# Merge stage of a decoder layer: routing in steps between the next quarter's half column blocks, row weights applied on VectorE, output projection 512 columns wide

## The chip, the cores and the metric

The kernel runs on one core of a Trainium2 chip. The metric is the device time of one execution in microseconds (us), the median of several runs. The core has five engines that each work through their own list of instructions in order: TensorE (PE, matrix products; its weight loads are listed apart as PEld), VectorE (DVE), ScalarE (ACT), GpSimd (POOL) and SyncE (SP). An instruction waits at the head of its engine's list until the semaphores it names are set, and all behind it on that engine wait with it. Transfers are issued from an engine's list (here from SP and POOL) and run on the DMA engines.

## The reference, cut to what matters

One decoder layer over 2048 tokens of width 1024. Two token mixers run side by side, differential attention (`attn`) and a causal convolution module (`c`); gates merge them, and a hierarchical mixture of experts (4 groups of 8, top 1 group, top 2 experts) and a gated per-layer embedding follow:

```
y_a = attn.reshape(B, S, ATTN_WIDTH) @ w_attn_out[i]
y_b = c @ w_conv_out[i] + b_conv_out[i]
gates = jax.nn.sigmoid(g + b_gate[i])
merged = gates[..., :D] * y_a + gates[..., D:] * y_b
h = h + merged @ w_o[i]
t = rmsnorm(h, norm_ffn[i]).reshape(B * S, D)
moe = hierarchical_moe(t, w_router_group[i], b_router_group[i],
                       w_router_expert[i], b_router_expert[i], w1[i], w3[i], w2[i])
h = h + moe.reshape(B, S, D)
ple_gate = jax.nn.sigmoid(rmsnorm(h, norm_ple[i]) @ w_ple_gate[i] + b_ple_gate[i])
h = h + ple_gate * (p[i] @ w_ple_proj[i])
```

## The kernel before

The kernel has five stages: mix (input projection, convolution, gates), attention, merge, the experts (moe) and the embedding (ple). The change lies in merge, which runs from about 1216 to 1715 us, and in the last steps that prepare the experts' gather. Every large product is made from float32 split into a high and a low part (`split`: the high part by a copy on ACT, the low part by a subtraction on DVE, L91 and L92) and three products (`mm3`, L96 to L98: high x high, low x high, high x low).

**Merge** handles the tokens in 4 quarters of 512. For each quarter the inputs of both branches are loaded and split (`bah`/`bal` for attention, whose rows are also scaled by a broadcast product `aR`, and `bch`/`bcl` for convolution). Then come 8 column blocks `j` of 128 output columns. In each, PE makes two groups of 12 products 128x512, one for each branch, into an accumulator `mps` (3 buffers); DVE applies the gates (L738 to L740), and the merged block is split into `mh` (ACT) and `ml` (DVE). Weights come as units of 512 KB, loaded on SP into `eraw` and split into `ewh` and `ewl`; `fetch` takes the next unit ahead of its use (`MERGE_W` gives the number of raw and split buffers).

The second half of a quarter is the **output projection**: 4 column parts `cc` of 256, and for each 4 token tiles `t`, 24 products 128x256 into `mps`; DVE adds the result to the residual rows `hq` (L756), and ACT sums the squares (`junk`). Two steps later (`LOGITS_AFTER`, a list of things to do, `todo`) `logits` transposes pieces of `hq` (`tps`, `hT`) and makes the router's products `lp`.

Then `merge_tail` computes the norm weight `r` (`h_std`), the logits `L`, and writes the normed rows: for each of 4 tiles ACT copies `hq` times `r` into `tt` (two buffers, L810), POOL multiplies by the gain `gffn` (L811) and issues the store to `T` (L812); the 2 MB store of `hq` itself to `HD` (L813) goes the same queue. `route` is a long chain of small DVE operations (group maximum, first and second expert, L833 to L859), a prefix count on PE (`pre`, L862 to L864), codes and eight pairs of masks `oh` and `ob` on DVE (L886, L888), and eight products that add to the dispatch table `tab` (L889).

After the fourth quarter `pick` turns the table into the gather's index: copy `tabs`, transposes `tps` (L928), products `dps` (L933), then `free`, `dst` and `idx`, and POOL gathers rows `xs` from `T` (L1231). `project` makes 96 products `pps` of 128x512 for the last stage, which don't depend on the routing, and stores them as PJ from POOL (L969). The first product of the experts reads the gathered rows after transposes (`tps` L1246, `ups` L1269).

Merge is not written in the order in which it runs: a framework's scheduler places each instruction on its engine's list, by what it depends on and by its priority in program order, so code of one quarter can stand in the list among that of the next. From the experts on the order is a fixed table, and the change leaves it as it is.

## Time and profile before

| | us |
|---|---|
| median of 3 runs (lowest, highest) | 2820.81 (2819.80, 2825.62) |
| the profiled execution | 2816.46 |
| its span in the trace | 2814.7 |
| PE busy in the span | 2661.8 |
| DVE, ACT, POOL busy | 1986.5, 1471.0, 405.6 |

The time is that of a whole execution; the span runs from the first to the last instruction recorded, so 1.76 us lie around it. The engines work side by side, and busy times are not to be added. A busy time says little by itself: where two engines wait for each other in turn, neither is busy all the time.

### The profile page before, as it was taken

The numbers are of one execution on the slowest core, as the hardware profiler recorded it, in microseconds if no ns is written. First come the engines' busy times: TensorE is split into PE (matmuls) and PEld (weight loads), VectorE is DVE, ScalarE is ACT, GpSimd is POOL, SyncE is SP. The second block draws the span as 40 slices with busy tenths as digits, with TensorE's granted clock in tenths as the row PEclk, the third lists the DMA queues.
The fourth block names the chain that finished last, engine by engine and source line by source line (L and its number), as shares of the span: only waits on it lengthen the run. The fifth ranks groups of instructions, "written<-read, shape, count | busy, mean of one in ns | idle before, by whom it ended". The sixth has DMA issues, their size and how long they took to land. (4 is left out here: it accounts for less than half of the span.)

```text
span 2814.7 us, 38600 instructions
## 1 busy us (share of the span) xinstructions
PE 2661.8 (95%) x13910; PEld 2209.8 (79%) x13911; DVE 1986.5 (71%) x3006; ACT 1471.0 (52%) x2700; POOL 405.6 (14%) x311
## 2 busy tenths in 40 slices
PE   7999999999999999989999998999999999999897
PEld 5898977898778878879789796667667777777776
DVE  6996238997787888864856746577777777775454
ACT  5232344233666666644544435566766766665333
POOL 2011122023210000000110112111111211111121
PEclk9999999999999999999999998999999999999999
DMA  5133444134433324164745637778888887885462
GB/s 191 64 113 113 139 164 150 60 124 151 164 96 103 115 76 122 37 218 150 239 161 172 210 130 270 249 281 307 294 282 301 316 316 283 314 296 182 149 209 91
DMA packets 177828, 520.83 MB, mean 185 GB/s; under 512 B 19120, under 2 KB 48576, under 8 KB 177120
## 3 DMA queue, kind: packets, MB, share of 16 engines
q1 hardware_dynamic: 135536, 397.02, 42.2%
q0 software_dynamic: 23664, 83.54, 8.0%
q10 hardware_dynamic: 18432, 37.76, 3.5%
q8 instruction: 110, 1.80, 0.3%
q14 instruction: 86, 0.70, 0.1%
HBM read 417.58 MB, written 100.66 MB: 184 GB/s over the span
## 5 line engine op out<-in xcount | busy, mean ns | idle before, releaser
L92 DVE TENSOR_TENSOR ewl<-eraw,ewh 128x1024 fp32r<-128x1024 f32 x464 | 549.5, 1219 | 140.7 <-ACT ewh L91 138.5
L91 ACT ACTIVATE ewh<-eraw 128x1024 fp32r<-128x1024 f32 x464 | 468.5, 1052 | 64.6 <-PE mps L97 27.2
L387 DVE SCALAR_TENSOR_TENSOR co<-cb,pvt,co 128x1024 f32<-128x1024 f32 x240 | 312.2, 1338 | 1.6
L96 PE MATMUL ps<-uh,wh 128*128 128x512 f32 x576 | 232.4, 406 | 4.3 <-ACT uh L91 4.3
L586 DVE TENSOR_REDUCE nm<-sc 128x1 f32<-128x512 f32 (+3 forms) x320 | 185.0, 605 | 62.0 <-PE sc L583 47.9
L97 PE MATMUL ps<-ul,wh 128*128 128x512 f32 x576 | 228.5, 398 | 0.0
L98 PE MATMUL ps<-uh,wl 128*128 128x512 f32 x576 | 227.3, 396 | 0.0
L1269 PE MATMUL ups<-ewh,xt 128*128 128x512 f32 x480 | 194.7, 406 | 5.5 <-ACT ewh L91 5.3
L1270 PE MATMUL ups<-ewl,xt 128*128 128x512 f32 x480 | 189.5, 395 | 2.1 <-DVE ewl L92 2.1
L96 PE MATMUL ps<-wh,uh 128*128 128x384 f32 x512 | 173.0, 338 | 0.0
L98 PE MATMUL ps<-wh,ul 128*128 128x384 f32 x512 | 172.1, 336 | 0.0
L97 PE MATMUL ps<-wl,uh 128*128 128x384 f32 x512 | 172.0, 336 | 0.0
L1207 POOL DMA_INDIRECT Y<-y,dst x49 | 66.4, 1355 | 657.2 <-ACT y L1077 483.1
L96 PE MATMUL mps<-ewh,mh 128*128 128x256 f32 x512 | 149.8, 293 | 3.0 <-ACT mh L91 3.0
L97 PE MATMUL mps<-ewl,mh 128*128 128x256 f32 x512 | 145.3, 284 | 0.0
L98 PE MATMUL mps<-ewh,ml 128*128 128x256 f32 x512 | 144.8, 284 | 0.0
L96 PEld LDWEIGHTS ps<-uh,wh 128*128 128x128 f32 x576 | 109.0, 190 | 32.5 <-ACT uh L91 5.0
L97 PEld LDWEIGHTS ps<-ul,wh 128*128 128x128 f32 x576 | 109.1, 189 | 28.7 <-issue 1.9
L1272 PE MATMUL ups<-ewh,xt 128*128 128x512 f32 x480 | 129.6, 392 | 0.0
L98 PEld LDWEIGHTS ps<-uh,wl 128*128 128x128 f32 x576 | 108.7, 189 | 26.3
L582 PE MATMUL sc<-Kt,Qt 128*128 128x512 f32 (+2 forms) x320 | 126.3, 401 | 3.2 <-ACT pr L572 2.8
L91 ACT ACTIVATE ah<-tp 128x512 fp32r<-128x512 f32 x144 | 82.5, 603 | 82.3 <-PE tp L632 68.5
(338 smaller groups left out, 6922.1 us busy)
## 6 DMA issues: line engine op xcount, KB each, us to landing
eraw<-in_we SPq DMA_DIRECT2D x384, 512.0 KB, 5.4
G<-sg POOLq DMA_DIRECT2D x64, 256.0 KB, 2.9
eraw<-in_wac SPq DMA_DIRECT2D x32, 512.0 KB, 4.1
ga<-G SPq DMA_DIRECT2D x32, 512.0 KB, 4.9
eraw<-in_wo SPq DMA_DIRECT2D x32, 512.0 KB, 3.7
ys<-Y SPq DMA_DIRECT2D x32, 512.0 KB, 7.2
wraw<-in_wqkv SPq DMA_DIRECT2D x16, 768.0 KB, 4.4
wraw<-in_wg SPq DMA_DIRECT2D x20, 512.0 KB, 3.9
```

The costliest lines, as they stand in the source:

```text
L91: nc.scalar.activation(hi, x, AF.Copy)
L92: (lo_eng or nc.vector).tensor_tensor(lo, x, f32(hi), ALU.subtract)
L96: nc.tensor.matmul(ps, lh, rh, start=start, stop=False)
L97: nc.tensor.matmul(ps, lh, rl, start=False, stop=False)
L98: nc.tensor.matmul(ps, ll, rh, start=False, stop=stop)
L387: nc.vector.scalar_tensor_tensor(acc, cb[:, i : i + HALF], wi, acc, ALU.mult, ALU.add)
L582: nc.tensor.matmul(sc[:, :n], Qt[:, 2 * m, qs], ks, start=True, stop=False)
L586: nc.vector.tensor_reduce(nm[:, qi, m, c : c + 1], sc[:, :w], AX.X, ALU.max, negate=True)
L1207: self.nc.gpsimd.indirect_dma_start(out=self.Y[:, :], out_offset=bass.IndirectOffsetOnAxis(ap=dst[R], axis=0), in_=y[R], in_offset=None)
L1269: self.nc.tensor.matmul(ps, xt[:, k, :P], wk[0], start=k == 0, stop=False)
L1270: self.nc.tensor.matmul(ps, xt[:, k, :P], wk[1], start=False, stop=False)
L1272: self.nc.tensor.matmul(ps, xt[:, k, P:], wk[0], start=False, stop=k == NK - 1)
```

## The change

It has four parts.

1. The output projection makes products 512 columns wide: 2 column parts instead of 4, 24 products for each tile and part as before, into a full accumulator. The units of `wo` are cut another way for it, and the right operand of a product is two runs of 256 columns of one unit. `take` replaces `fetch`, and six split buffers replace five. `logits` is called for each tile and part, after one step instead of two.
2. `merge_tail`, `route`, `pick`, `project` and `projected` become generators. In the next quarter one step of routing is written after each of the two groups of a column block, and what is left of it before the next branch. In the last quarter routing and `pick` alternate with the steps of `project`.
3. The row store no longer uses ACT and POOL: one DVE operation (`rows_out`, L833 of the changed kernel) makes `tt` from `hq`, `r` and `gffn`. The store to `HD` is written ahead of those to `T`.
4. The capacities `caps`, 32 memsets on DVE in `pick`, are set once on POOL at the start.

```
@@ -39,8 +39,8 @@
 PR_BUFS = 11
 QK_AFTER = 10
 LN_AFTER = (4, 9)
-LOGITS_AFTER = 2
-MERGE_W = (2, 5)
+LOGITS_AFTER = 1
+MERGE_W = (2, 6)
 AHEAD = 5
 EARLY = 4
 MOE_W = (8, 14)
@@ -139,6 +139,9 @@
         self.idx = cp.tile([P, NBLK * NE], I32, name="idx")
         self.slots = cp.tile([1, 3, NE], I32, name="slots")
         self.over = cp.tile([1, 1], I32, name="over")
+        self.caps = cp.tile([1, NE], F32, name="caps")
+        for e in range(NE):
+            self.nc.gpsimd.memset(self.caps[:, e : e + 1], float(sum(SLOTS[e])))
         self.xp = self.ctx.enter_context(self.tc.tile_pool(name="xp", bufs=2, reuse_waits="tile"))
 
     def consts(self, cp):
@@ -657,12 +660,14 @@
             px = ctx.enter_context(tc.tile_pool(name="mpx", bufs=2, space=PSUM, reuse_waits="tile"))
             pr = ctx.enter_context(tc.tile_pool(name="mpr", bufs=1, space=PSUM, reuse_waits="tile"))
             self.mp, self.sp, self.pp, self.px, self.pr = mp, sp, pp, px, pr
-            units = [A["wac"][j] for j in range(NK)] + [A["wo"][i] for i in range(NK)]
+            wo = A["wo"].rearrange("(a c m) p (h x) -> a m h p c x", c=2, m=2, h=2)
+            units = [A["wac"][j] for j in range(NK)] + [wo[a, m, h] for a in range(2) for m in range(2) for h in range(2)]
             units, ready = units * 4 + halves(A["wpp"]) + halves(A["pT"][0]), []
 
-            def fetch():
-                if units:
+            def take(n, ahead=MERGE_W[1] - 4):
+                while units and len(ready) < n + ahead:
                     ready.append(self.unit(units.pop(0)))
+                return [ready.pop(0) for _ in range(n)]
 
             def load(j, q):
                 ga = sp.tile([P, 2, 512], F32, name="ga", tag="ga", bufs=3)
...
@@ -735,38 +738,47 @@
                         for k in range(4):
                             self.mm3(ps, wh[:, m, k, :], wl[:, m, k, :], br[m][0][:, k, :], br[m][1][:, k, :], k == 0, k == 3)
                         y.append(ps)
+                        if q:
+                            next(routing, None)
                     nc.vector.tensor_tensor(ga[:, 0, :], y[0], ga[:, 0, :], ALU.mult)
                     nc.vector.scalar_tensor_tensor(ga[:, 1, :], y[1], self.pv("b_co", j), ga[:, 1, :], ALU.add, ALU.mult)
                     nc.vector.tensor_tensor(ga[:, 0, :], ga[:, 0, :], ga[:, 1, :], ALU.add)
                     self.split(mh[:, j, :], ml[:, j, :], ga[:, 0, :])
                     ga = nga
+                if q:
+                    for _ in routing:
+                        pass
                 if q < 3:
                     bq = [branch(self.AT, q + 1, "ba"), branch(self.CT, q + 1, "bc")]
-                for cc in range(4):
-                    fetch()
-                    fetch()
-                    w = [tuple(x.rearrange("p (k c) -> p k c", k=4) for x in ready.pop(0)) for _ in range(2)]
+                for cc in range(2):
+                    w = [tuple(x.rearrange("p (c k j) -> p k c j", c=2, k=2) for x in u) for u in take(4)]
                     for t in range(4):
-                        ps = pp.tile([P, 512], F32, name="mps", tag="mps")[:, :256]
+                        ps = pp.tile([P, 512], F32, name="mps", tag="mps")
                         ts = slice(t * P, (t + 1) * P)
                         for k in range(NK):
-                            wh, wl = w[k // 4]
-                            self.mm3(ps, mh[:, k, ts], ml[:, k, ts], wh[:, k % 4, :], wl[:, k % 4, :], k == 0, k == NK - 1)
-                        hs = hq[:, t, cc * 256 : (cc + 1) * 256]
+                            wh, wl = w[k // 2]
+                            self.mm3(ps.rearrange("p (c j) -> p c j", c=2), mh[:, k, ts], ml[:, k, ts], wh[:, k % 2], wl[:, k % 2], k == 0, k == NK - 1)
+                        hs = hq[:, t, cc * 512 : (cc + 1) * 512]
                         nc.vector.tensor_tensor(hs, ps, hs, ALU.add)
-                        junk = sp.tile([P, 256], F32, name="junk", tag="junk")
+                        junk = sp.tile([P, 512], F32, name="junk", tag="junk", bufs=1)
                         nc.scalar.activation(junk, hs, AF.Square, accum_out=ss[:, t, cc : cc + 1])
                         self.step()
-                        if t % 2:
-                            self.todo.append([LOGITS_AFTER, lambda cc=cc, t=t, hq=hq, lp=lp: self.logits(cc, t - 1, hq, lp)])
+                        self.todo.append([LOGITS_AFTER, lambda cc=cc, t=t, hq=hq, lp=lp: self.logits(cc, t, hq, lp)])
+                if q == 3:
+                    work = self.project(take)
                 while self.todo:
                     self.step()
-                self.merge_tail(q, hq, ss, lp)
-            for _ in range(4):
-                fetch()
-            self.pick()
+                    if q == 3:
+                        next(work)
+                routing = self.merge_tail(q, hq, ss, lp)
+            for _ in range(3):
+                next(work)
+            for steps in (routing, self.pick()):
+                for _ in steps:
+                    next(work, None)
             self.first = [self.gather(self.idx[:, b * NE : b * NE + 1]) for b in range(2)]
-            self.project(ready)
+            for _ in work:
+                pass
 
     def wait(self, x, after):
         self.tc.add_manual_dep(x.ins, after.ins.name, mybir.DependencyInfo(mybir.DependencyClass.Sync, mybir.DependencyReason.DATA))
...
@@ -804,14 +815,24 @@
         L = sp.tile([P, 4, NG + NE], F32, name="L", tag="L", bufs=1)
         nc.vector.tensor_tensor(L, lp, r.unsqueeze(2).to_broadcast([P, 4, 36]), ALU.mult)
         nc.vector.tensor_tensor(L, L, self.bc[:, :36].unsqueeze(1).to_broadcast([P, 4, 36]), ALU.add)
+        nc.gpsimd.dma_start(self.HD[q * 512 : (q + 1) * 512, :].rearrange("(t p) d -> p t d", p=P), hq)
+        store = self.rows_out(q, hq, r)
+        if q < 3:
+            yield from store
+            yield from self.route(q, L)
+        else:
+            for _ in self.route(q, L):
+                next(store, None)
+                yield
+
+    def rows_out(self, q, hq, r):
+        nc, sp = self.nc, self.sp
         for t in range(4):
             a = q * 512 + t * P
             tt = sp.tile([P, D], F32, name="tt", tag="tt")
-            nc.scalar.activation(tt, hq[:, t, :], AF.Copy, scale=r[:, t : t + 1])
-            nc.gpsimd.tensor_tensor(tt, tt, self.gffn, ALU.mult)
+            nc.vector.scalar_tensor_tensor(tt, hq[:, t, :], r[:, t : t + 1], self.gffn, ALU.mult, ALU.mult)
             nc.gpsimd.dma_start(self.T[a : a + P, :], tt)
-        nc.gpsimd.dma_start(self.HD[q * 512 : (q + 1) * 512, :].rearrange("(t p) d -> p t d", p=P), hq)
-        self.route(q, L)
+            yield
 
 
     def route(self, q, L):
@@ -841,15 +862,20 @@
         gmax, m1, m2 = (self.tops[:, i, q * 4 : q * 4 + 4] for i in range(3))
         V.tensor_reduce(gmax, gl, AX.X, ALU.max)
         og = first(gl, gmax, NG)
+        yield
         V.tensor_tensor(self.gl[:, q * 4 : q * 4 + 4, :], gl, bc(gmax, (4, NG), 2), ALU.subtract)
         es, ev, ev2 = new(4, NG, EPG), new(4, EPG), new(4, EPG)
         V.tensor_tensor(es, el, bc(og, (4, NG, EPG), 3), ALU.mult)
         V.tensor_reduce(ev, es.rearrange("p t g e -> p t e g"), AX.X, ALU.add)
...
+        yield
         pre = self.pr.tile([P, 5, NE], F32, name="pre", tag="pre")
         for t in range(4):
             nc.tensor.matmul(pre[:, t + 1 :, :], self.onesb, bc(Sb[:, t, :], (4 - t, NE), 1), start=t == 0, stop=False)
         nc.tensor.matmul(pre[:, 1:4, :], self.trib, Sb[:, 1:, :], start=False, stop=False)
         nc.tensor.matmul(pre[:, 0, :], self.trib, Sb[:, 0, :], start=False, stop=True)
+        yield
         code = new(4, NE)
         V.tensor_tensor(code, pre[:, :4, :], bc(self.base, (4, NE), 1), ALU.add)
         V.tensor_tensor(self.base, pre[:, 4, :], self.base, ALU.add)
         V.scalar_tensor_tensor(code, code, float(NE), bc(self.iota[:, :NE], (4, NE), 1), ALU.mult, ALU.add)
+        yield
         ck = new(4, 2)
         for k in range(2):
             tmp = new(4, NE)
             V.tensor_tensor(tmp, E[k], code, ALU.mult)
             V.tensor_reduce(ck[:, :, k], tmp, AX.X, ALU.add)
+        yield
...
@@ -880,12 +911,16 @@
         for t in range(4):
+            made = []
             for k in range(2):
                 i = 8 * q + 2 * t + k
                 oh = sp.tile([P, P], F32R, name="oh", tag="oh", bufs=3)
                 V.tensor_scalar(oh, self.iota, mf[:, t, k : k + 1], None, ALU.is_equal)
                 ob = sp.tile([P, NBLK * NE], F32R, name="ob", tag="ob")
                 V.tensor_scalar(ob, self.rc[:, : NBLK * NE], bf[:, t, k : k + 1], self.tokm[:, i : i + 1], ALU.is_equal, ALU.mult)
+                made.append((i, oh, ob))
+            yield
+            for i, oh, ob in made:
                 nc.tensor.matmul(self.tab, oh, ob, start=i == 0, stop=i == 2 * NT - 1)
 
 
...
@@ -955,17 +994,21 @@
             ps = pool.tile([P, 512], F32, name="pps", tag=tag)
             for k in range(2):
                 a = t % 4 * 256 + k * P
-                (ph, pl), (wh, wl) = pt[t % 8 // 4], w[k]
+                (ph, pl), (wh, wl) = pt, w[k]
                 ks, ns = slice(a, a + P), slice(n * 512, (n + 1) * 512)
                 self.mm3(ps, ph[:, ks], pl[:, ks], wh[:, ns], wl[:, ns], k == 0, k == 1)
             self.nc.scalar.copy(o[:, n * 512 : (n + 1) * 512], ps)
-
-    def project(self, parts):
-
-        for t, tag in zip(range(0, 8, 2), ("bch", "bcl") * 2):
+            yield
+
+    def project(self, take):
+
+        w = take(2)
+        for t, tag in zip(range(0, NT // 2, 2), ("bch", "bcl") * 2):
+            if t % 4 == 0:
+                pt, = take(1)
             o = self.mp.tile([P, 2, D], F32, name="pj", tag=tag)
             for i in range(2):
-                self.projected(t + i, parts[2:], parts[:2], self.pp, "mps", o[:, i, :])
+                yield from self.projected(t + i, pt, w, self.pp, "mps", o[:, i, :])
             self.nc.gpsimd.dma_start(self.PJ[t * P : (t + 2) * P, :].rearrange("(i p) d -> p i d", p=P), o)
 
 
```

The scheduler turns this into new lists; three places follow. The numbers at the start of a row are line numbers of the kernel, and `r_...` are the small tiles of routing.

On PE, where the second quarter's prefix count `pre` stands among the branch groups, before the change: behind the first quarter's projection there are four whole groups and nine products of the fifth ahead of it.

```order
L97 MATMUL mps<-bal,ewh 128x512
L98 MATMUL mps<-bah,ewl 128x512
L862 LDWEIGHTS onesb
L862 MATMUL pre<-r_12675,onesb 128x128
...
L864 LDWEIGHTS trib
L864 MATMUL pre<-r_12675,trib 128x32
L96 MATMUL mps<-bah,ewh 128x512
```

On PE, the same place after the change: 12 whole groups stand ahead of it.

```order
L96 MATMUL mps<-bch,ewh 128x512
L97 MATMUL mps<-bcl,ewh 128x512
L98 MATMUL mps<-bch,ewl 128x512
L890 LDWEIGHTS onesb
L890 MATMUL pre<-r_12683,onesb 128x128
...
L892 LDWEIGHTS trib
L892 MATMUL pre<-r_12683,trib 128x32
L96 MATMUL mps<-bah,ewh 128x512
```

The count has moved from within the third column block to behind the sixth; `tab`, which stood between the sixth and the eighth group, now stands behind all sixteen, among `aR` and the first projection products.

On DVE, the start of the second quarter before the change, from the norm weight on: `ga` is a column block's gate step, all other rows are logits and routing.

```order
L802 TENSOR_REDUCE htot<-hss 128x4
L189 RECIPROCAL h_std<-h_std 128x4
L738 TENSOR_TENSOR ga<-mps,ga 128x512
L805 TENSOR_TENSOR L<-lp,h_std 128x144
L806 TENSOR_TENSOR L<-L,bc 128x144
L842 TENSOR_REDUCE cst<-L 128x4
L833 TENSOR_TENSOR r_12641<-L,cst 128x16
L844 TENSOR_TENSOR gl<-L,cst 128x16
L835 SCALAR_TENSOR_TENSOR r_12641<-r_12641,cst 128x16
L836 TENSOR_REDUCE r_12643<-r_12641 128x4
L837 TENSOR_TENSOR r_12642<-r_12641,r_12643 128x16
L846 TENSOR_TENSOR r_12649<-L,r_12642 128x128
```

On DVE, the same place after the change, from the logits on: the stores' `tt` and the gate steps stand here now, and routing begins behind them.

```order
L816 TENSOR_TENSOR L<-lp,h_std 128x144
L833 SCALAR_TENSOR_TENSOR tt<-hq,h_std,gffn 128x1024
L817 TENSOR_TENSOR L<-L,bc 128x144
L833 SCALAR_TENSOR_TENSOR tt<-hq,h_std,gffn 128x1024
L743 TENSOR_TENSOR ga<-mps,ga 128x512
L744 SCALAR_TENSOR_TENSOR ga<-mps,pvt,ga 128x512
L92 TENSOR_TENSOR ewl<-eraw,ewh 128x1024
L745 TENSOR_TENSOR ga<-ga 128x512
L743 TENSOR_TENSOR ga<-mps,ga 128x512
L833 SCALAR_TENSOR_TENSOR tt<-hq,h_std,gffn 128x1024
L92 TENSOR_TENSOR ml<-ga,mh 128x512
L833 SCALAR_TENSOR_TENSOR tt<-hq,h_std,gffn 128x1024
```

The four operations for the store stand among the first three groups' gate steps, the third and fourth behind the first use of the third group's accumulator, and routing (L863 and on) behind the fourth.

On PE, the tail before the change, from the last table product on: PJ products (`pps`) stand between the steps of `pick`, and 25 more behind them.

```order
L889 MATMUL tab<-ob,oh 128x512
L96 MATMUL pps<-ewh 128x512
L97 MATMUL pps<-ewl,ewh 128x512
L98 MATMUL pps<-ewh,ewl 128x512
L96 MATMUL pps<-ewh 128x512
L97 MATMUL pps<-ewl,ewh 128x512
L928 MATMUL tps<-cst,tabs 128x128 x4
L940 MATMUL vp<-own,vals 1x32 x3
L98 MATMUL pps<-ewh,ewl 128x512
L96 MATMUL pps<-ewh 128x512
L97 MATMUL pps<-ewl,ewh 128x512
L933 MATMUL dps<-bd,turned 128x128 x4
```

On PE, the tail after the change: PJ products end ahead of the table, and nothing stands between the steps.

```order
L96 MATMUL pps<-ewh 128x512
L97 MATMUL pps<-ewl,ewh 128x512
L98 MATMUL pps<-ewh,ewl 128x512
L924 MATMUL tab<-ob,oh 128x512 x2
L981 MATMUL vp<-own,vals 1x32 x3
L924 MATMUL tab<-ob,oh 128x512 x6
L967 MATMUL tps<-cst,tabs 128x128 x4
L973 MATMUL dps<-bd,turned 128x128 x4
L1289 MATMUL tps<-cst,xs 128x128 x16
L1312 MATMUL ups<-ewh,xt 128x512
```

Of the 96 PJ products 34 stood ahead of `pre` in the tail, and 72 stand there now; the other 24 stand between `pre` and `tab`. On POOL all four PJ stores now stand ahead of the first gather, where two stood behind it.

## Rows read from the trace of the kernel before

**Rows 1.** The page's first part: engine busy us (share) xinstructions.

```profile
PE 2661.8 (95%) x13910; PEld 2209.8 (79%) x13911; DVE 1986.5 (71%) x3006; ACT 1471.0 (52%) x2700; POOL 405.6 (14%) x311
```

**Rows 2.** Windows: length, busy (count) PE, PEld, DVE, ACT, POOL; clock, DMA share, GB/s.

```profile
1338.50:1393.60 55.10, 50.30 (x227) 40.48 (x226) 46.81 (x95) 26.76 (x33) 12.84 (x9) 0.97 0.74 255
...
1672.30:1720.50 48.20, 36.70 (x165) 28.78 (x163) 31.78 (x96) 20.22 (x32) 18.44 (x16) 0.85 0.60 220
```

**Rows 3.** Waits of PE, 1200 to 1740: total us, times, longest us.

```profile
PE pre L862 <- DVE r L859: 18.0, 4, 4.6
PE tab L889 <- DVE ob L888: 4.3, 3, 3.8
...
PE mps L96 <- ACT mh L91: 3.0, 1, 3.0
```

**Rows 4.** PE's timeline, second quarter: start us, us, engine, line, operation, wait.

```profile
1346.43 0.39 PE L96 MATMUL mps<-bah,ewh 128*128 128x512 f32 x1
1346.65 0.39 PE L97 MATMUL mps<-bal,ewh 128*128 128x512 f32 x1
...
1358.61 0.42 PE L862 MATMUL pre<-r,onesb 128*128 128x128 bf16 x4 [4.54 <-DVE r L859]
...
1360.41 0.63 PE L96 MATMUL mps<-bch,ewh 128*128 128x512 f32 x1
1360.83 0.63 PE L97 MATMUL mps<-bcl,ewh 128*128 128x512 f32 x1
```

**Rows 5.** DVE's groups by form, 1338.5 to 1393.6: busy us, mean ns.

```profile
L833 DVE TENSOR_TENSOR r<-L,cst 128x16 f32<-128x16 f32 x1 | 2.1, 2067 | 0.0
L856 DVE TENSOR_TENSOR r<-r,r 128x128 f32<-128x128 f32 x2 | 2.1, 1027 | 0.0
L806 DVE TENSOR_TENSOR L<-L,bc 128x144 f32<-128x144 f32 x1 | 1.4, 1385 | 0.0
...
L805 DVE TENSOR_TENSOR L<-lp,h_std 128x144 f32<-128x144 f32 x1 | 0.3, 298 | 0.0
```

**Rows 6.** Groups by line, whole span: busy us, mean ns, idle before.

```profile
L811 POOL TENSOR_TENSOR tt<-tt,gffn 128x1024 f32<-128x1024 f32 x16 | 39.3, 2467 | 46.0 <-ACT tt L810 46.0
...
L1361 DVE SCALAR_TENSOR_TENSOR hn<-h,p_std,gb 128x1024 f32<-128x1024 f32 x16 | 21.9, 1368 | 0.5
```

**Rows 7.** DVE's timeline, second quarter, then the tail.

```profile
1360.52 2.39 DVE L868 SCALAR_TENSOR_TENSOR r<-r,cst 128x128 f32<-128x128 f32 x1
...
1678.39 2.25 DVE L837 TENSOR_TENSOR r<-r,r 128x16 f32<-128x16 f32 x1
...
1710.82 0.43 DVE L937 TENSOR_SCALAR idx<-dst 128x512 int32<-128x512 int32 x1
```

**Rows 8.** POOL's timeline, second quarter, then the tail.

```profile
1339.64 0.76 POOL L813 DMA_DIRECT2D HD<-hq  x1 [118.84 <-DVE hq L756]
...
1360.15 2.62 POOL L811 TENSOR_TENSOR tt<-tt,gffn 128x1024 f32<-128x1024 f32 x1 [1.67 <-ACT tt L810]
...
1713.79 0.76 POOL L969 DMA_DIRECT2D PJ<-pj  x1
```

**Rows 9.** PE's timeline in the first quarter's output projection.

```profile
1321.06 0.28 PE L97 MATMUL mps<-ewl,mh 128*128 128x256 f32 x1
...
1323.69 0.28 PE L98 MATMUL mps<-ewh,ml 128*128 128x256 f32 x1
```

**Rows 10.** PE's timeline in the tail.

```profile
1671.60 0.28 PE L98 MATMUL mps<-ewh,ml 128*128 128x256 f32 x1
...
1686.77 0.42 PE L862 MATMUL pre<-r,onesb 128*128 128x128 bf16 x4 [4.21 <-DVE r L859]
...
1720.55 0.77 PE L1269 MATMUL ups<-ewh,xt 128*128 128x512 f32 x1
```

**Rows 11.** DMA issues, 1338.5 to 1353: count, KB each, us to landing.

```profile
HD<-hq POOLq DMA_DIRECT2D x1, 2048.0 KB, 10.7
```

**Rows 12.** The tile tt: its transfers to T, whole span.

```profile
DMA to landing us min/median/max: 3.0/3.6/9.1
```

More of the change, by code (lines that the diff above doesn't have):

```diff
@@ L718, in merge @@
                 for j in range(NK):
-                    fetch()
+                    w, = take(1)
                     if j + 1 < NK:
@@ L729, in merge @@
                         self.wait(x, gate)
-                    wh, wl = (x.rearrange("p (m k c) -> p m k c", m=2, k=4) for x in ready.pop(0))
+                    wh, wl = (x.rearrange("p (m k c) -> p m k c", m=2, k=4) for x in w)
                     gate = nc.scalar.activation(ga, ga, AF.Sigmoid)
@@ L785, in logits @@
         for i in range(4):
-            k = cc * 2 + i % 2
-            nc.tensor.transpose(ps[:, i * P : (i + 1) * P], hq[:, t + i // 2, k * P : (k + 1) * P], self.ident)
+            k = cc * 4 + i
+            nc.tensor.transpose(ps[:, i * P : (i + 1) * P], hq[:, t, k * P : (k + 1) * P], self.ident)
         hT = sp.tile([P, 512], F32, name="hT", tag="hT")
@@ L792, in products @@
             for i in range(4):
-                k = cc * 2 + i % 2
-                first, last = cc == 0 and t == 0 and i == 0, cc == 3 and t == 2 and i == 3
-                nc.tensor.matmul(lp[:, t + i // 2, :], hT[:, i * P : (i + 1) * P], self.wr[:, k, :], start=first, stop=last)
+                first, last = cc == 0 and t == 0 and i == 0, cc == 1 and t == 3 and i == 3
+                nc.tensor.matmul(lp[:, t, :], hT[:, i * P : (i + 1) * P], self.wr[:, cc * 4 + i, :], start=first, stop=last)
         self.todo.append([1, products])
@@ L864, in route @@
         nc.tensor.matmul(pre[:, 0, :], self.trib, Sb[:, 0, :], start=False, stop=True)
+        yield
         code = new(4, NE)
@@ L911, in pick @@
         V.tensor_reduce(mine, tmp, AX.X, ALU.add)
+        yield
         V.tensor_scalar(tmp, row, mine, None, ALU.is_lt)
@@ L917, in pick @@
         V.scalar_tensor_tensor(slot, rank, 2.0, slot, ALU.mult, ALU.add)
+        yield
         own, bd = new("own", NE), new("bd", 4, NE)
@@ L925, in pick @@
         V.tensor_copy(vals[:, 2:3], nb)
+        yield
         tp = self.px.tile([P, N], F32, name="tps", tag="tps")
@@ L930, in pick @@
         V.tensor_copy(turned, tp)
+        yield
         dp = self.px.tile([P, N], F32, name="dps", tag="tps")
@@ L941, in pick @@
         V.tensor_copy(self.slots[:, :2, :], vp[:1, :2, :])
-        caps, again, over = new("caps", NE), new("again", NE), new("over", 1)
-        for e in range(NE):
-            V.memset(caps[:1, e : e + 1], float(sum(SLOTS[e])))
-        V.tensor_tensor(again[:1], vp[:1, 1, :], caps[:1], ALU.is_gt)
+        again, over = new("again", NE), new("over", 1)
+        V.tensor_tensor(again[:1], vp[:1, 1, :], self.caps, ALU.is_gt)
         V.tensor_tensor(again[:1], again[:1], vp[:1, 2, :], ALU.mult)
@@ L1343, in projection @@
             else:
-                self.projected(t, pt, wpp, self.ed, "ed", pj[t])
+                for _ in self.projected(t, pt[t % 8 // 4], wpp, self.ed, "ed", pj[t]):
+                    pass
         def combined(i):
```

11 lines of the change are left out of this document (7 added, 4 removed).

## The prediction

> **What bounds the kernel now.** I read the page's first part first: TensorE (PE) is busy for 95% of the span [rows 1], so a gain must come either from fewer PE microseconds or from stretches in which PE stands still. The windows view was next, for the stage that the change touches. The first half of the second quarter (from the last output-projection product of one quarter to the end of the branch blocks of the next) takes 55.10 us with PE busy for 50.30 at a mean clock of 0.97; VectorE (DVE) is busy for 46.81 of it, far more than in the other stretches, so DVE is nearly as loaded as PE there. The tail (last output projection to the first expert) takes 48.20 us with PE busy for 36.70 at 0.85 [rows 2]. The waits view says what PE waits for in this stage: 18.0 us in four waits for the routing's bf16 mask ahead of `pre`, 4.3 in three for `ob` ahead of `tab` (3.8 of it once), and 3.0 once for the last `mh` [rows 3]. That is about 25 us of stall in 2,816. PE's timeline shows what a stall costs beyond itself: before the wait 128x512 products start 0.22 to 0.23 us apart, after the 4.54 us wait 0.42 to 0.43 us, the lower of the two clock levels [rows 4]; some six products run so before the spacing is back.
>
> Why is DVE late at `pre`? Its groups by form show operations far slower than their size: a 128x16 product 2.07 us, a 128x128 one 2.39, two 128x128 with a mean of 1.03, a 128x144 sum 1.39, where another 128x144 operation takes 0.30 [rows 5, 7]. The routing chain of tiny operations is what holds PE, and it is stretched. In the timeline each of the long ones lies in a stretch in which GpSimd (POOL) multiplies rows by `gffn` (2.47 us each, 39.3 in all [rows 6]): the one of 2.39 us begins at 1360.52, 0.37 behind the start of a product on POOL at 1360.15 [rows 7, 8].
>
> **The change, part by part.**
>
> *Output projection 512 wide.* 256-wide products start 0.1195 us apart (22 steps from 1321.06 to 1323.69 [rows 9]), 512-wide branch products 0.2275 [rows 4]. A pair of 24-product groups took 2 x 24 x 0.1195 = 5.74 us and becomes 24 x 0.2275 = 5.46. That is 0.28 for each of 8 pairs in 4 quarters: **-8.8**. Bounds: 0 if a right operand in two 256-wide pieces is read like two products, -8.8 if not; the nearest rows are the 512-wide ones with one piece, so I take -8.8. The Trainium skill ("TensorE: Matmul & The Clock Gate", Back-to-back issue gap) gives an isolated gap of columns / 2.4 GHz + 2.5 ns, so 109 and 216 ns; both rows lie above it (119.5 and 227.5), and by that rule the gain would be 24 x 2.5 ns x 32 = about 2 us, an estimate from the page. The measured rows decide.
>
> *Row store on DVE.* Sixteen ScalarE copies and sixteen POOL products go; sixteen DVE operations 128x1024 come. The nearest row, a scalar-tensor-tensor of that shape in a later stage, takes 1.368 us [rows 6], so DVE gets 4 x 1.37 = 5.5 us more for a quarter. It loses the stretching: with 0.30 as the undisturbed price, (2.39 - 0.30) + (2.07 - 0.30) + 2 x (1.03 - 0.30) + (1.39 - 0.30) = 6.4. So DVE's first half is 46.81 - 6.4 + 5.5 = 45.9 us: hardly changed in sum, but the lost time no longer lies inside the routing chain. The Trainium skill ("SBUF — State Buffer", SBUF: two separate sides) says that a DVE operation with two SBUF inputs and a GpSimd operation that reads SBUF lock one shared port pair against each other; the stretched rows agree with it in place, and no run here yet shows the same operations with POOL idle.
>
> *Routing in steps.* In the new order `pre` stands behind 12 of the 16 branch groups where it stood behind 4 groups and 9 products, so PE reaches it 144 x 0.2275 = 32.8 us into the half instead of 57 x 0.2275 = 13. DVE needed about 17.5 us for the chain up to there (13 plus the wait of 4.5), so it now has 15 us to spare and this wait goes. `tab` moves behind all 16 groups, among the next branch's transposes and the first projections. At each of three boundaries what is lost today is (18.0 - 4.2) / 3 = 4.6 of stall [rows 3, 10] plus 6 x 0.2 = 1.2 of low clock [rows 4], 5.8 in all. What is late next is DVE: 45.9 us of work against a PE that needs 55.1 - 5.8 = 49.3, and its last operations are the `ob` masks for `tab`. I take a third of the gain as lost again there or to the weights' `ewl` split queued behind them, 4.0 kept: 3 x 4.0 = **-12**, between 0 and -17.4.
>
> *Waits that the store adds.* `tt` has two buffers. The third DVE store waits until the first T transfer has landed, and everything behind it on DVE (the gate products that free PE's three accumulators, routing) waits too. T stands behind the 2 MB HD transfer on POOL's queue, issued at 1339.64 and 10.7 us under way [rows 8, 11], so the first T lands at about 1352.5; DVE comes to the third store behind the third group, at about 1350. A wait of some 2.5 us: PE has three accumulators, so two groups of 2.7 us cover it. Price 0; without the cover it is 2.5 at each boundary.
>
> *First projection.* In the first quarter PE waits 3.0 for the eighth block's `mh` [rows 3]. The first group now takes 21 x 0.2275 = 4.8 us instead of 2.5 until it needs that block, so 2.3 of the wait goes, and with it part of the low clock behind it: **-3**, between 0 and -4.2 (3.0 + 1.2).
>
> *Tail.* From the last projection product (1671.60) to the first expert product (1720.55) 48.95 us pass; `pre` starts after 15.2, the index is ready after 39.65 [rows 7, 10]. After the change 72 PJ products (16.4 us) and the logits' 3 to 4 us stand ahead of `pre`, so it comes at about 20.4, 5 later, although the chain itself loses a stretched operation of 2.25 [rows 7] and the next behind it. From there nothing stretches (the 3.8 wait of `tab` goes [rows 3]), `tab` products wait for no PJ products in between, and neither do the two transposing steps: 4 us to the first `ob`, 6 for the six that remain and pick's small operations, 6.5 from `tab` to the index, which gives about 37.5, 2 earlier. POOL issues all PJ stores ahead of the gathers, where one stood behind the first two (1713.79 [rows 8]): 1 to 2 more. **-3.5**, between -6 and +4 (`pre` later by 5, with 1 given back).
>
> *Start of the stage.* Loads change places, and 32 memsets leave DVE: **-1**, between -3 and +2. Weights: the four wo units of a projection are split ahead of it in DVE's order, so the larger take costs nothing; its cover is the last branch blocks, and without it one load and split, some 3 us a quarter.
>
> **Sum.** -8.8 - 12 - 3 - 3.5 - 1 = -28.3. The profiled execution took 2816.46 us, 1.76 more than its span, and lies 4.35 below the median of the runs shown. 2816.46 - 28.3 = 2788.2, and on the median's scale 2792.5.
>
> **Rivals.**
>
> *The stall comes back at `tab`.* DVE's load of 45.9 against 49.3 is thin. If it arrives 5 us late at the end of the half, PE stalls there as long as it does now at `pre`, with the same low clock. For it: `tab` stands directly ahead of the first projections, DVE also splits the next branch's inputs there. Against it: the chain starts no later than before. Then only the wider products and the small terms remain: 2820.8 - 8.8 - 1 to 2 = about 2810.
>
> *The wider products give nothing* (two pieces), the rest as forecast: 2792.5 + 8.8 = about 2801.
>
> *Slower: DVE stands behind the store.* One place: the third `tt` waits for T behind HD. Beyond the two covered groups (5.4 us) each microsecond stops PE at three boundaries. T's slowest landing so far is 9.1 us, its median 3.6 [rows 12]. If HD and T shared the queues with the weights so that T landed 16 us after its issue, the stall is some 9 us a boundary with 1.2 of low clock: 3 x (10 - 4.6 - 1.2) = +13 against the loss of today, with -8.8 still there: about 2825. It decides from a stall of about 9 us; a landing nearly twice the slowest seen is needed.
>
> *The tail gets longer*, since `pre` stands behind 72 products: +4 instead of -3.5, so 2800.
>
> **How the numbers follow.** Forecast (projection gain, most of the stall): 0.60. Two pieces: 0.10. Tail longer: 0.10. Stall back at `tab`: 0.15, of which a third ends within 0.2% (5.6 us, about what a measurement of this kernel can tell from no change). Slower by the store: 0.05. The range reaches from all bounds at their best (-8.8 - 17.4 - 4.2 - 6 - 3 = -39, 2781) to the returned stall, 2810. Faster 0.88, same 0.08, slower 0.04. The likeliest one's own range is 2784 to 2800.
>
> **What the changed profile would show.** Right: PE waits for `pre` near 0 in three of four, at most 2 us at `tab`; routing operations of 128x128 at 0.3 us with POOL without products; 512-wide `mps<-ewh,mh` 0.2275 apart; the first half at about 51 us; the tail at about 45. Wrong: `hq` products at 0.24 us or more; DVE idle for over 5 us ahead of `tt`, released by T; a new row of PE waits for `ob` or `ewl`; `pre` over 21 us behind the last projection with no shorter remainder.

## The result and the profile after

The changed kernel takes 2792.98 us (median of 4 runs, 2790.53 to 2795.52) against 2820.31 for the kernel before on the same chips: a ratio of 0.9901, interval 0.9883 to 0.9919. The forecast was 2792.5. The sum was right, but the experiments show that its largest term stood under the wrong heading.

The page's first part and the waits of TensorE (PE) in the merge stage, to be held against [rows 1, 3]:

```profile
PE 2644.6 (95%) x13142; PEld 2163.0 (78%) x13143; DVE 1971.9 (71%) x2958; ACT 1446.6 (52%) x2620; POOL 369.8 (13%) x327
```

```profile
PE tab L924 <- DVE ob L920: 8.5, 8, 2.6
PE tps L1289 <- DMA xs<-T,idx: 7.2, 1, 7.2
```

No wait for the prefix count `pre` is left (18.0 us in four before). The table products `tab` wait instead, 2.3 to 2.6 us at the end of each half.

Windows of the second quarter's first half, its projection, and the tail (columns as in [rows 2]):

```profile
1330.30:1377.90 47.60, 47.60 (x232) 39.59 (x230) 36.48 (x78) 21.54 (x27) 2.90 (x5) 1.00 0.84 287
1377.90:1436.30 58.40, 55.48 (x283) 46.00 (x282) 31.75 (x51) 25.27 (x41) 0.00 (x0) 1.00 0.41 128
1645.10:1692.23 47.13, 36.76 (x179) 28.72 (x177) 27.10 (x99) 16.50 (x28) 8.69 (x12) 0.83 0.66 246
```

PE is busy in every microsecond of the first half now, at the full clock. VectorE (DVE) is busy for 36.48 us of it, where it was 46.81 of 55.10 [rows 2].

DVE's groups by form in the second quarter (busy us, mean ns; compare [rows 5, 6]):

```profile
L833 DVE SCALAR_TENSOR_TENSOR tt<-hq,h_std,gffn 128x1024 f32<-128x1024 f32 x4 | 5.1, 1278 | 0.0
L882 DVE TENSOR_TENSOR r<-r,r 128x128 f32<-128x128 f32 x2 | 0.6, 286 | 0.0
L817 DVE TENSOR_TENSOR L<-L,bc 128x144 f32<-128x144 f32 x1 | 0.3, 301 | 0.0
L854 DVE TENSOR_TENSOR r<-L,cst 128x16 f32<-128x16 f32 x1 | 0.2, 167 | 0.0
```

The stretched operations are back at their size (0.17, 0.29 and 0.30 us where it was 2.07, 1.03 and 1.39), and a row store costs 1.28 us.

PE's timeline in a projection, and at the two ends of the tail with the count between them (start, duration; compare [rows 9, 10]):

```profile
1383.37 0.39 PE L98 MATMUL mps<-ewh,ml 128*128 128x512 f32 x1
1383.60 0.39 PE L96 MATMUL mps<-ewh,mh 128*128 128x512 f32 x1
1383.83 0.39 PE L97 MATMUL mps<-ewl,mh 128*128 128x512 f32 x1
...
1645.01 0.40 PE L98 MATMUL mps<-ewh,ml 128*128 128x512 f32 x1
...
1665.15 0.32 PE L890 MATMUL pre<-r,onesb 128*128 128x128 bf16 x4
...
1692.23 0.78 PE L1312 MATMUL ups<-ewh,xt 128*128 128x512 f32 x1
```

The wide products start 0.23 us apart, so the right operand in two pieces is read at the rate of one piece. The tail takes 1692.23 - 1645.01 = 47.2 us, where it took 48.95; its count starts 20.1 us behind the projection, and its index is ready at 37.9:

```profile
1682.50 0.43 DVE L977 TENSOR_SCALAR idx<-dst 128x512 int32<-128x512 int32 x1
```

From such starts the stage can be cut into pieces in every run. In us, from the start of a quarter's last projection product to that of the next quarter's last branch product (half), and from there to the last projection product (proj); the quarters are q0 to q3, and the rest runs from the first expert product to the end of the span:

| | q0 proj | q1 half + proj | q2 half + proj | q3 half + proj | tail | rest |
|---|---|---|---|---|---|---|
| before | 59.6 | 55.6 + 56.8 | 55.6 + 56.0 | 55.7 + 54.1 | 48.9 | 1094.2 |
| after | 52.4 | 47.4 + 58.4 | 47.4 + 58.4 | 47.4 + 55.7 | 47.2 | 1098.0 |

The eight `tab` products and the wait ahead of them have moved from the half to the projection, so the two are taken together: -6.6, -5.8 and -6.6 us in the three quarters, -7.3 in the first projection, -1.7 in the tail: -28.0. With -0.3 ahead of the table and +3.8 in the rest this is the difference of the two spans, 2814.7 to 2790.2. The rest of the program (experts and embedding, unchanged) took 1092.2 to 1099.0 us in the fourteen profiles of this study, so +3.8 lies within its spread and is not put down to the change.

### The profile page after: what moved, and what is told of

Read it like the earlier page. It is cut to its first block, busy times and chain, and to the rows that moved or that the text cites. A ratio compares the mean times of both kernels' runs of the same rounds, so it can differ in the third digit from the quotient of the medians.

```text
span 2790.2 us, 36893 instructions
## 1 busy us (share of the span) xinstructions
PE 2644.6 (95%) x13142; PEld 2163.0 (78%) x13143; DVE 1971.9 (71%) x2958; ACT 1446.6 (52%) x2620; POOL 369.8 (13%) x327
## 5 line engine op out<-in xcount | busy, mean ns | idle before, releaser
L92 DVE TENSOR_TENSOR wl<-wraw,wh 128x1024 fp32r<-128x1024 f32 (+1 forms) x50 | 77.3, 1548 | 64.4 <-ACT wh L91 58.8
L575 ACT ACTIVATE pr<-sc,top 128x512 f32<-128x512 f32 (+3 forms) x176 | 109.2, 631 | 20.2 <-DVE top L596 20.1
L422 ACT COPY qk<-ps 128x256 f32<-128x256 f32 x64 | 23.9, 373 | 179.9 <-PE ps L98 143.1
```

The source lines that it names most:

```text
L92: (lo_eng or nc.vector).tensor_tensor(lo, x, f32(hi), ALU.subtract)
L575: nc.scalar.activation(pr[c][:, m, : ws[c]], scs[c][:, : ws[c]], AF.Exp, bias=top, accum_out=sums[:, qi, m, c : c + 1])
```

## The experiments

All times are medians, with the ratio to the kernel before and its interval. The kernel before ran beside each group of runs, with medians of 2817.2 to 2820.3 us, so a difference between two runs is worked out from their ratios (0.001 is 2.8 us); an interval is some 5 us to either side.

**1. Routing at once.**

```
 routing = self.merge_tail(q, hq, ss, lp)
+if q < 3:
+    for _ in routing: pass
```

> The changed kernel, but each quarter's routing is written out at once behind its norm weights and not in steps between the half blocks; wide projection and row store on VectorE stay. In the instruction lists the prefix count then stands behind 102 branch products of the next quarter (23.2 us) and not 144, and the table products among the last 70 branch products, ahead of the end of the half. Theory 1 (what counts is whether VectorE's chain, free of the GpSimd products, ends before TensorE reaches its place): the chain needed 17.5 us with the stretch, loses some 4.4 of it and gets 5.1 of row stores, so it is ready at about 18 to 20 and no wait at the prefix count returns (under 1 us each); the waits of 2.6 us for the table masks at the end of each half shrink to under 1. Time 3 to 8 us below the changed kernel. Rival (the steps themselves remove the stall): 3 to 5 us of wait for the mask at three boundaries with low clock behind, time 10 to 17 us above the changed kernel.

2791.38 us, 0.9902 (0.9885 to 0.9918). The changed kernel without its steps in the first three boundaries is as fast (0.9902 against 0.9901). At `pre` PE waits 1.7 us in three, where it was 13.8 before, and the table masks are in time:

```profile
PE pre L893 <- DVE r L888: 1.7, 3, 1.0
```

```profile
1362.97 0.50 PE L927 MATMUL tab<-ob,oh 128*128 128x512 f32 x1
```

The table's first product starts 33.2 us behind the first quarter's projection, without a wait; in the changed kernel it starts at 50.5 and waits 2.6 us for its mask. So the wait at `tab` is one that the steps bring: they put the masks 17 us later. With the row store on DVE the rival, the steps as the cause, falls. The promised 3 to 8 us less did not show either.

**2. Row store back on ScalarE and GpSimd.**

```
-nc.vector.scalar_tensor_tensor(tt, hq[:, t, :], r[:, t:t+1], self.gffn, ALU.mult, ALU.mult)
+nc.scalar.activation(tt, hq[:, t, :], AF.Copy, scale=r[:, t:t+1])
+nc.gpsimd.tensor_tensor(tt, tt, self.gffn, ALU.mult)
```

> The changed kernel with the row store back on ScalarE (copy) and GpSimd (product by the gain); steps and wide projection stay. Theory 1: routing operations that run beside a GpSimd product take 1.4 to 2.4 us again instead of 0.17 to 0.30; the prefix count, 33 us into the half, hides that (no wait there), while the table masks come 1 to 2 us later than now or as now (6.4 of stretch against 5.1 of row stores less on VectorE). Tail: up to 4 us more, as two GpSimd products fall on the masks. Time 2 to 9 us above the changed kernel. Rival 'place alone': GpSimd's products cost nothing, time within 2 us. Rival 'contention alone': waits of over 3 us at the prefix count come back, time over 10 us above.

2819.1 us, 0.9996 (0.9984 to 1.0008): the whole gain is gone, far beyond what I expected. PE does not wait at `pre`, but for the gate steps that free its accumulators, and at `tab` (PE's waits in the merge stage; `tab` was 8.5 in the changed kernel):

```profile
PE mps L96 <- DVE ga L743: 14.6, 8, 3.8
PE tab L925 <- DVE ob L921: 10.3, 8, 2.1
...
PE mps L96 <- DVE ga L744: 3.7, 3, 1.4
```

GpSimd's timeline, two products merged in one row (the second runs from 1341.06 to 1343.53), and DVE's beside it:

```profile
1338.69 4.84 POOL L834 TENSOR_TENSOR tt<-tt,gffn 128x1024 f32<-128x1024 f32 x2 [4.53 <-ACT tt L833]
```

```profile
1338.71 0.69 DVE L743 TENSOR_TENSOR ga<-mps,ga 128x512 f32<-128x512 f32 x1 [1.39 <-PE mps L98]
1339.32 1.95 DVE L817 TENSOR_TENSOR L<-L,bc 128x144 f32<-128x144 f32 x1
1341.19 3.42 DVE L92 TENSOR_TENSOR ewl<-eraw,ewh 128x1024 fp32r<-128x1024 f32 x1
```

The sum `L` takes 1.95 us (0.30 alone) and the weight split 3.42 (1.22 alone), while a gate step that reads PSUM and SBUF takes its 0.69. The split begins 0.13 us into the second product and ends 1.08 us behind that product's end, so it was held once, until the product was over.

**3. Narrow pieces.**

```
-self.mm3(ps.rearrange("p (c j) -> p c j", c=2), ..., wh[:, k % 2], wl[:, k % 2], ...)
+for c in range(2):    # outside the loop over k
+    self.mm3(ps[:, c*256:(c+1)*256], ..., wh[:, k % 2, c], wl[:, k % 2, c], ...)
```

> The changed kernel, but each 24-product group of the projection is made as two groups of 24 products 256 columns wide into the two halves of the accumulator. By the spacing of the rows before (0.1195 against 0.2275) +8.8 us, and the first projection waits for its last block again (+2.4 to +4): 11 to 13 above the changed kernel. By the length of the projection stretches in the changed kernel's trace, from which I work out some 2.9 us a quarter, +11.6 and 14 to 16 in all. If wide products in two pieces gave nothing: within 1 us but for the first wait.

2804.66 us, 0.9944 (0.9926 to 0.9962): 12 above the changed kernel. The first projection is 6.9 us longer, the three pairs of half and projection 3.6, 3.2 and 5.0, the tail 0.8 shorter. Not all of the 6.9 is the width: in this first projection PE waits 2.1 us for a weight part `ewl` and 0.8 for an `ewh`, not for the last block. A wait for `ewl` of 1.9 to 2.3 us stands there in runs 10 and 11 too, and their wide first projections take 55.7 and 57.4 us, against 52.4 in the changed kernel and 59.3 here.

**4. Memsets later.** The loop over `caps` is moved from the start of the program into `constants()` of the merge stage.

> The changed kernel with the 32 memsets of the capacities on GpSimd in the merge stage, where GpSimd has nothing to do, and not ahead of all else. In the changed kernel's trace TensorE waits 1.2 us for a low part from GpSimd near the start, and the merge stage begins 1.0 us later than before. If the memsets cause that: the merge stage begins 1.0 us earlier and the time is about 1 us lower (not to be told apart by the timing, but by the trace). If not: the stage begins at the same time.

2796.24 us, 0.9922 (0.9904 to 0.994), if anything above the changed kernel. The merge stage's first `aR` product starts at 1222.54 here and at 1223.52 in the changed kernel, but in the fourteen profiles this start lies between 1219.8 and 1224.9 wherever the memsets are (1224.33 in run 10, which has this edit too). Inconclusive.

**5 and 6. The two halves of the row store apart.** ScalarE's copy with DVE's product, and a product on GpSimd alone, which leaves out the gain:

```
+nc.scalar.activation(tt, hq[:, t, :], AF.Copy, scale=r[:, t:t+1])       # 5
+nc.vector.tensor_tensor(tt, tt, self.gffn, ALU.mult)
```

```
+nc.gpsimd.tensor_tensor(tt, hq[:, t, :], r[:, t:t+1].to_broadcast([P, D]), ALU.mult)   # 6
```

> The changed kernel with the row store split: ScalarE copies the row times its norm weight, VectorE (not GpSimd) multiplies by the gain. So ScalarE's four copies a quarter are back in order ahead of the gates' sigmoid, and GpSimd's products are not. Theory P (the stretching of VectorE by GpSimd's products is what the store back on GpSimd cost): no stretched operation, time within 5 us of the changed kernel, about 2793 to 2798. Theory A (ScalarE's copies hold up the sigmoid and with it the gate steps): waits of TensorE for the gate step of 2 to 4 us at the first blocks return, time 2805 to 2820.

> The changed kernel with the row store on GpSimd alone: one product of the row by its norm weight (read as a broadcast); the gain is left out, so that GpSimd does four products a quarter as before and ScalarE none. Theory P: VectorE's operations beside the products take 1.5 to 3.4 us again, waits for the gate step and the table masks return, time 2810 to 2820. Theory A: stretched operations but no waits for the gate step, since the sigmoid stands early on ScalarE; time 2793 to 2800.

2800.74 us, 0.9935 (0.9917 to 0.9954), and 2801.64 us, 0.9945 (0.9926 to 0.9964). Neither theory alone: the copies cost 10 us over the changed kernel (0.9935 - 0.9901), the GpSimd products 12, and the two together, in run 2, 27, within the intervals the sum of both (a product takes 1.9 us in run 6 and 2.4 in run 2). Waits of PE in run 5, then in run 6:

```profile
PE tab L925 <- DVE ob L921: 10.2, 3, 3.9
```

```profile
PE tab L924 <- DVE ob L920: 8.2, 8, 1.8
...
PE mps L96 <- DVE ga L744: 3.6, 3, 1.8
```

Without GpSimd's products no DVE operation is stretched in run 5, and the wait for gate steps is gone. PE waits for masks once a boundary, longer at a time than in the changed kernel (up to 3.9 us against 2.6), and the granted clock of the three pairs of half and projection is 0.97 to 0.98 where it was 1.00: these pairs are 1.5, 2.8 and 2.2 us longer, of which 1.1, 1.8 and 1.3 are PE's own busy time. With the products and without the copies, stretched operations (1.8 us for a 128x16 one) and the wait for gate steps return; the wait at `tab` is what it was (8.2 us against 8.5).

**7 and 8. One part alone.** Run 3's edit with run 1's (of the three, only the row store is new in the first three quarters), and run 2's with run 1's (only the wide projection). The scheduler's lists differ from those before in both.

> The row store on VectorE as the only one of the three parts within the first three quarters: projection in pieces of 256 columns, routing at once, the tail as in the changed kernel. If the steps are worth nothing, as the run with routing at once suggests: at the level of the run with narrow pieces, 2800 to 2808. If the steps matter where the projection is narrow: 2810 or more.

> The wide projection as the only one of the three parts within the first three quarters: row store on ScalarE and GpSimd, routing at once, the tail as in the changed kernel. If parts add up: before less the 11.7 us that narrow pieces cost, 2806 to 2810. If steps together with the store on GpSimd were harmful: this, and the run with the store on GpSimd at 2819 is explained by the steps. If the wide products' gain is lost in the waits that the store makes (TensorE only comes earlier to the same wait): 2814 to 2820.

2804.49 us, 0.9953 (0.9938 to 0.9968): within 3 us of run 3, so the steps are worth nothing that can be told beside the narrow projection too. The wide projection alone: 2823.06 us, 1.002 (1.0008 to 1.0032), no faster than before, even a little slower. Waits of PE in run 8:

```profile
PE pre L894 <- DVE r L889: 16.7, 3, 6.1
PE mps L96 <- DVE ga L744: 12.4, 3, 4.4
```

In three boundaries it waits 16.7 us for `pre` (13.8 before, [rows 3, 10]) and 12.4 for gate steps. The four projections are 1 to 6 us shorter, but PE loses more than that in the halves, which take 62 to 63 us instead of 56 at a clock of 0.94 to 0.95 over half and projection. The chain is not the one of before: 77 branch products stand ahead of `pre` in this list instead of 57, and `pre` still waits; it starts 32 us behind the projection, where it was 21. On DVE a weight split takes 3.42 us and a gate step 3.10 (0.68 alone) beside GpSimd's products. So here the wide products' gain is lost to waits for DVE.

Run 8 differs from run 2 in the steps alone, and from run 1 in the row store alone. With the store on GpSimd the steps are worth some 7 us by the medians (1.0020 - 0.9996, interval 2 to 12) and 2 by the pieces of the stage; the store, with routing at once, is worth 33 (1.0020 - 0.9902).

**9. One line.** Run 2's edit the other way round, in the kernel before; nothing else is changed.

> The kernel before with one edit: the row store's ScalarE copy and GpSimd product become the one VectorE operation; projection 256 wide, routing at once, the old tail. If the store is what the change earns with: 2802 to 2808, the level of the two runs with narrow pieces (2804.5 and 2804.7), waits at the prefix count of under 2 us in three of four, no stretched operation. If it needs the steps or the wide projection beside it: 2812 to 2820.

2800.8 us, 0.9933 (0.9918 to 0.9948). The one line gives 18 to 19 us: by the pieces 3.5, 2.2 and 4.6 in the three boundaries and 6.6 in the tail. PE's timeline at the end of its projection, at `pre`, and at the first expert product:

```profile
1663.23 0.28 PE L98 MATMUL mps<-ewh,ml 128*128 128x256 f32 x1
...
1676.34 0.30 PE L861 MATMUL pre<-r,onesb 128*128 128x128 bf16 x4
...
1705.60 0.77 PE L1268 MATMUL ups<-ewh,xt 128*128 128x512 f32 x1
```

With the old order of the tail, `pre` comes 13.1 us behind the projection and the tail takes 42.4 us, against 48.95 before and 47.2 in the changed kernel.

**10 and 11. An earlier tail, without and with the steps.** On top of run 1 and 4 (10), and of 4 alone (11):

```
-for _ in range(3): next(work)
 for steps in (routing, self.pick()):
-    for _ in steps: next(work, None)
+    for i, _ in enumerate(steps):
+        if i % 2: next(work, None)
...
+# q == 3: the HD store is issued behind the fourth tt
```

> A version meant to be faster: routing at once, memsets late, and in the tail two edits: PJ products taken at every second step, so that 53 and not 72 stand ahead of the last prefix count, and the last HD store behind the T stores, so that the third and fourth row store don't wait 2.8 and 1.7 us for T. The last prefix count then comes about 15.5 us and not 20.1 behind the last projection product, and the tail takes 43 to 45 us and not 47 to 48.5: 2786 to 2789. If the tail is held by the gather and not by the count: 2790 to 2793, tail at 47 or more.

> As the run before it, but with routing in steps as in the changed kernel, so that the two differ in the steps alone. By the two earlier pairs (1.6 us with the wide projection, 0.2 with the narrow one) the steps are worth nothing: within 3 us of the run before it. If steps help once the rest is short: 4 us or more below it.

2781.08 us, 0.9858 (0.9839 to 0.9877), the fastest of this study and 12 below the changed kernel; and 2788.68 us, 0.9887 (0.9871 to 0.9903). PE's timeline of run 10:

```profile
1645.68 0.40 PE L98 MATMUL mps<-ewh,ml 128*128 128x512 f32 x1
...
1661.52 0.32 PE L896 MATMUL pre<-r,onesb 128*128 128x128 bf16 x4
...
1681.62 1.94 PE L1295 MATMUL tps<-cst,xs 128*128 128x128 f32 x8 [5.76 <-DMA xs<-T,idx]
...
1686.48 0.78 PE L1318 MATMUL ups<-ewh,xt 128*128 128x512 f32 x1
```

The count comes at 15.8 us and the tail takes 40.8 (40.7 in run 11). Two things changed in it, the number of PJ products ahead of the count and the place of the HD store; they were not tried apart. The two runs differ in the steps alone: half and projection sum to 103.9, 104.3 and 103.8 us without them, to 106.7, 107.4 and 105.1 with them, where PE waits 7.8 us in three for the table masks again. Here the steps cost about 8 us (0.9887 - 0.9858), 7.2 by these sums; the granted clock of the three pairs is 0.98 with them and 1.00 without.

**12. Row store twice.** The operation is written twice in a row.

> The changed kernel with each row store's VectorE operation done twice: 5.1 us more for VectorE at each boundary, nothing else. If VectorE is what the end of a half waits for (my reading of the 2.6 us waits for the table masks): those waits grow to 5 to 8 us at three boundaries, time 8 to 16 us above the changed kernel. If it has room (38.9 us busy in 49.7): waits as now, time within 4 us.

2788.78 us, 0.9893 (0.9875 to 0.9911): not slower, 2 us below the changed kernel, which can't be told from none. The window of the second quarter's first half, and PE's wait for the masks:

```profile
1328.80:1377.60 48.80, 48.80 (x241) 40.50 (x240) 41.99 (x85) 22.55 (x29) 2.90 (x5) 1.00 0.80 279
```

```profile
PE tab L925 <- DVE ob L921: 1.5, 5, 0.6
```

```profile
1379.24 0.51 PE L925 MATMUL tab<-ob,oh 128*128 128x512 f32 x1 [0.64 <-DVE ob L921]
```

The same product in the changed kernel:

```profile
1380.67 0.96 PE L924 MATMUL tab<-ob,oh 128*128 128x512 f32 x2 [2.62 <-DVE ob L920]
```

DVE takes 5.1 us more, and PE is still busy throughout. The first `tab` product starts 50.5, 50.2 and 51.9 us behind the three projections, against 50.5, 50.1 and 50.4 in the changed kernel, so 5.1 us more work put its mask at most 1.5 us later: DVE had room. The wait is shorter because PE comes later, in the second quarter by 2 us: the half is 1.2 us longer, and eight of the next branch's transposes (1.0 us) now stand ahead of `tab`. That `tab` starts at 50.5 at all is the steps' doing (33.2 in run 1).

## Why the prediction came out right, and where it was wrong

Place by place the sum fits. In the three boundaries the forecast has -12 and three quarters of the wide term, -18.6, and -19.0 was measured; in the first projection -5.2 and -7.3; in the tail -3.5 and -1.7; at the start -1 and -0.3. By cause it does not fit, and with an interval of 5 us to either side the agreement of the total within 0.5 us is luck. (The chances of the single outcomes add up to 0.90 faster, 0.05 same and 0.05 slower, not the 0.88, 0.08 and 0.04 of the last line.) Point by point:

- **Row store on DVE**: priced at nothing for the sum ("hardly changed in sum"). This is the step that failed. Alone it gives 18 to 19 us (run 9); taken away it costs 27 (run 2). The cause of the stretched chain was read rightly and is shown: operations at their size in every run without GpSimd products (but for one mask of 0.28 us that took 0.5 in runs 9 to 11), stretched in runs 2, 6 and 8. But its gain was entered under the steps. The Trainium skill ("SBUF — State Buffer", SBUF: two separate sides) names what is stretched: DVE operations with two SBUF inputs, against a GpSimd operation that reads SBUF, and those in a 2-port mode. The traces agree for the first kind: `ewl` (two SBUF inputs) took 3.42 instead of 1.22, `ga<-mps,ga` with one input in PSUM 0.69 beside a product too. Masks of one tensor input were held as well: in the tail before, `oh` took 2.40 instead of 0.28 and `ob` 2.58 instead of 0.54.
- **Routing in steps**: -12, measured nothing with the store on DVE (run 1 against the changed kernel 0, run 7 against run 3 within 3) or a loss (run 11 against 10: 8 slower). There the chain is ready even at the early place. With the store on GpSimd the later place trades the wait at `pre` (16.7 us in run 8) for longer ones at the gate steps and at `tab` (run 2), a gain of some 7 us by the medians and 2 by the pieces.
- **What the ScalarE copies hold up** was not in the prediction at all. The row store on ScalarE and DVE instead of DVE alone costs some 10 us (run 5), 6.5 of it in the three boundaries. The gates, weight splits and `mh` pass through ScalarE in order, and four copies stand among them; the second quarter's first `mh` is done 16.4 us behind the projection instead of 12.6. By what the later masks are late there, the copies' own 1.14 us each or what they wait for (3.8 us in all for `T`), was not measured.
- **Wide projection**: -8.8, measured 12 and 14 (run 3 against the changed kernel, run 7 against run 1), 6.9 and 4.6 of it in the first quarter, where the forecast had -3 apart for the wait for the last block. The two terms together, 11.8, fit within the interval; how they divide is open, since a wait for `ewl` stands in the first quarter of runs 3 and 7. That the gain can be lost to waits for DVE (run 8) was not foreseen. The isolated gap of the Trainium skill ("TensorE: Matmul & The Clock Gate", Back-to-back issue gap), from which the prediction worked out an estimate of 2 us, does not fit: the measured spacings decide.
- **DVE as the next bound** ("I take a third of the gain as lost again there"): waits of up to 2.6 us at `tab` came as said, but for another reason: the steps put the masks late (run 1), and a doubled store cost nothing (run 12). DVE's first half, forecast at 45.9 us, took 36.48, since much of the routing now stands behind the half; over half and projection 71.1 became 68.2.
- **Waits that the store adds**: price 0, right, but the covered wait of 2.5 us at each boundary did not come: no T transfer took more than 7.9 us to land. DVE waits for T only in the tail (2.8 and 1.7 us), ahead of a count that came later anyway.
- **Tail**: -3.5, measured -1.7. `pre` at 20.1 (forecast 20.4) and the index at 37.9 (37.5) were right; the gather is not faster for the PJ stores ahead of it (from index to first expert product 9.3 us in both). The rival was sharper than I weighed it: with the same store the old order of the tail takes 42.4 us (run 9), 5 less, and its count comes at 13.1. The 72 products ahead of `pre` are the likely reason; run 9 differs in more than these.
- **Start of the stage**: -1, measured -0.3, within the spread.

## What to carry to other kernels

When an engine's small operations are slower than their size, take that apart first, by itself: one line gave two thirds of this gain. The same line is worth 18 to 19 us in the kernel before, 27 beside the steps and the wide projection, and 33 beside the wide projection with routing at once, so parts of a change aren't priced one by one. And work that fills an engine ahead of a critical product is only free while it ends before the product's input is ready: 19 filler products fewer, together with an HD store moved behind the row stores, took 6 us off the tail.

## What the runs showed of the hardware that was not expected

A DVE operation with two SBUF inputs that begins during a GpSimd product of 1.9 to 2.6 us is held until the product is over: 128x16 and 128x32 operations of under 0.2 us took up to 2.75 us (run 2, begun 0.3 us ahead of the recorded start of its product), and the split of 1.22 took 3.42 in three boundaries each of runs 2 and 8. In the merge stage 16 products stretched 16 operations in the kernel before and in runs 2 and 8. Reductions that began during such products took their 0.17 to 0.39 us, and gate steps that read PSUM their 0.69 and 0.74.

In this kernel 5.1 us more work on an engine that is 77% busy (36.48 of 47.60) cost nothing (run 12): `tab`, which waits for its mask, started at most 1.5 us later.
